# Letting the scheduler order TensorE's instructions in the layer 0 mixers of a two-layer hybrid backbone

## The chip, the cores and the metric

The program runs on one core of one Trainium2 chip. The metric is the device time of one execution in microseconds (us), the median of several runs. A profile of one execution stands beside it: the start and length of every instruction on the engines TensorE (PE, with its weight loads as PEld), VectorE (DVE), ScalarE (ACT) and GpSimd (POOL), and the transfers of the DMA queues.

## The reference, cut to what matters

640 tokens (128 of a context, 512 latent) of width 2048 go through two layers with a shared residual stream. Everything is float32.

```python
# per layer: (shift, scale, gate) = SiLU(cond) @ w_ada + b_ada ; h = RMSNorm(x) * (1 + scale) + shift
#            p = h @ w_in      (one projection for all head groups)
#            x = x + gate * ( concat(mixer_1(p) * silu(z_1), mixer_2(p) * silu(z_2)) @ w_out )
def delta_chunked(q, k, v, g, beta, s0):          # layer 0, mixer A: 8 heads, chunks of 64, both directions
    ...
    tmat = lmat + jnp.eye(CHUNK, dtype=F32)       # a triangular system in each chunk
    u = lax.linalg.triangular_solve(tmat, v * beta[..., None], ...)
    w = lax.linalg.triangular_solve(tmat, kb * jnp.exp(gc)[..., None], ...)
    def step(s, xs):                              # a serial scan over the chunks
        vn = ui - jnp.einsum('bhcd,bhde->bhce', wi, s)
        o = jnp.einsum('bhcd,bhde->bhce', qi * jnp.exp(gi)[..., None], s) + jnp.einsum('bhcs,bhse->bhce', ai, vn)
        s = s * jnp.exp(gl)[..., None, None] + jnp.einsum('bhcd,bhce->bhde', ki * ..., vn)
    ...
# layer 0, mixer B: 8 heads of windowed attention with a sink logit
# layer 1, mixers C (4 heads of gated linear attention) and D (8 heads of neighbourhood attention)
```

## The kernel before, in words

**Main work.** Each projection is cut into panels of 128 output columns; a panel is 16 blocks of 128 rows. Operands are split into a high and a low part, so that each block costs three matmuls of 320 tokens (`hh,w_hi`, `hl,w_hi`, `hh,w_lo`) for each half of the tokens, all adding up in a PSUM tile `acc`. A panel is thus 96 `acc` matmuls. Its weights come in quarters: a transfer into `w_st`, a cast on ACT into `w_hi` (L1048), a subtraction on DVE into `w_lo` (L1050); each of the three tiles has 3 buffers. `acc` has 3 buffers in PSUM, and a panel takes two of them. In layer 0, 53 panels make the mixers' inputs, and 16 more, the output projection, follow.

**The mixers of layer 0** run beside that main work as streams (Python generators, L1658 to L1733): convolutions, gates, preparation of a delta-net head (`a_prep`, L240), inversion of its triangular blocks on POOL (`a_invert`, L474, tiles `i_S`), joining the inverse (`a_join`), the serial scan (`a_scan`, L329), and the attention of a B head (`b_head`, L694, through `attn_run` and `attn_out`). A scan has ten steps for each head. A step first multiplies the state `a_s` by two stationary tiles (`a_st<-a_s,a_wT` and `a_st<-a_s,a_o`), ACT and DVE turn the result into `a_vno` (L411) and `a_vns` (L409), and TensorE then takes three products (`a_st<-a_r,a_Zt`, which belongs to the next step and reads `a_r` that ACT makes ahead, then `a_st<-a_vno,a_at` and `a_st<-a_vns,a_ktm`), from which DVE makes the next state (L426). In a B head each block of 128 queries has scores (`at_s`), a softmax, a transposition (`at_pt`), a copy on ACT into `at_P` (L614) and the product with the values (`at_o`).

**What sets the order.** The function `run` (L1202) is a planner that works while the program is written. It keeps an estimated time `g.now`, which each matmul advances, and the streams yield the time that they want to wait, from the table `LAT` (`hop=1.3` between two halves of a scan step, `pt=1.3` between `at_pt` and `at_o`, `inv=52` for an inversion). When no stream is due, `Main.step` issues three matmuls of main work. So the order in which matmuls are written interleaves scan steps with about a dozen `acc` matmuls each.

The framework then schedules the written program: at build time, with a timing model of its own, it gives out instructions as their inputs come free in that model, the earlier written one first among those that are ready. Each engine executes its own list in that order. Matmuls and transpositions go through two helpers (L74 and L83), which can tie each one behind the instruction of TensorE that was written before it:

```python
        i = self.nc.tensor.matmul(out, lhsT=lhsT, rhs=rhs, **kw)
        if self.pin:
            self.tc.keep_in_program_order(i)
```

With `g.pin` true, TensorE's list is the planner's order. It starts true (L1554), is set to false before the mixers of layer 1 (L1827), and is set to true in `out_proj` (L1535) after the first 14 panels of the output projection, ahead of the last two, which are done in halves. All other engines are ordered by the scheduler throughout.

After the mixers `out_proj` (L1502) finishes the output projection panel by panel: DVE adds each panel to the residual (`x`, L1518), and the vectors of the next layer's modulation (`ada_vec`, `scale` and `vec`, L1319) are computed on DVE, ACT and POOL as a filler.

Of the kernel before, what the change touches and what calls it, by code (L numbers as in the profile page):

```python
# [203 lines left out]
def a_conv(g, h, which, src):  # L204

    nc = g.nc
    pad = g.pad
    nc.scalar.copy(pad[:, 2:130], src[0][:, 0:128])
    nc.scalar.copy(pad[:, 134:326], src[0][:, 128:320])
    nc.scalar.copy(pad[:, 326:646], src[1])  # L210
    w = g.convw[:, which * 8 + h]
    y = g.pt.tile([128, CL], F32, name="a_y", tag="tmp")
    nc.vector.tensor_scalar_mul(y, pad[:, 0:CL], w[:, 0:1])
    for j in range(1, 5):
        nc.vector.scalar_tensor_tensor(out=y, in0=pad[:, j:j + CL], scalar=w[:, j:j + 1], in1=y,  # L215
                                       op0=ALU.mult, op1=ALU.add)
    t = g.pt.tile([128, CL], F32, name="a_t", tag="tmp")
    nc.scalar.activation(t, y, AF.Tanh, scale=0.5)
    o = (g.pa1 if which == 2 else g.pe).tile([128, T], F32, name=f"a_o{which}", tag=f"a_o{which}", bufs=(2, 2, 1)[which])
    nc.vector.scalar_tensor_tensor(out=o[:, 0:128], in0=t[:, 0:128], scalar=1.0, in1=y[:, 0:128], op0=ALU.add, op1=ALU.mult)  # L220
    for hf in range(2):
        nc.vector.scalar_tensor_tensor(out=o[:, 128:].rearrange("p (b a c) -> p a b c", a=2, c=64)[:, hf],
                                       in0=by_block(t[:, 132:], hf), scalar=1.0, in1=by_block(y[:, 132:], hf),
                                       op0=ALU.add, op1=ALU.mult)
    return o
# [332 lines left out]
def a_setup(g, es):  # L558

    nc, tc = g.nc, g.tc  # L560
    g.pa1 = es.enter_context(tc.tile_pool(name="pa1", bufs=1))
    g.paw = es.enter_context(tc.tile_pool(name="paw", bufs=1))
    g.Zt = [g.pa1.tile([128, 10, 64], F32, name=f"a_Zt{i}") for i in range(2)]
    g.pad = g.pa1.tile([128, CP], F32, name="a_pad")
    for z in g.Zt + [g.pad[:, 0:2], g.pad[:, 130:134], g.pad[:, 646:648]]:
        nc.gpsimd.memset(z, 0.0)
# [120 lines left out]
def b_query(g, h, qsrc):  # L687
    q = g.pb.tile([128, T], F32, name="b_q", bufs=2)
    drain(g, q, (yield from qsrc), SC)
    b_rope(g, q)  # L690
    return q
# [31 lines left out]
def b_setup(g, es):  # L723
    tc, nc = g.tc, g.nc
    g.pb = es.enter_context(tc.tile_pool(name="pb", bufs=1))
    t = g.pb.tile([128, 1536], F32, name="b_tab")
    nc.sync.dma_start(t, g.I["b_tab"])
    g.cos, g.sin, g.bmask = t[:, 0:512], t[:, 512:1024], t[:, 1024:1536]
# [473 lines left out]
def run(g, main, *streams):  # L1202


    live = [[s, None, g.now] for s in streams]
    while live:
        for e in live:
            if e[2] <= g.now if e[1] is None else e[1]():
                try:
                    y = next(e[0])  # L1210
                    e[1], e[2] = (y, 0) if callable(y) else (None, g.now + (y or 0))
                except StopIteration:
                    live.remove(e)
                break
        else:
            if not main.step():
                nn = min([e[2] for e in live if e[1] is None] + [main.when()])
                assert nn < INF
                g.now = nn
# [153 lines left out]
def ada_store(pool, n, k, width=512):  # L1373

    w = width // 4
    t = pool.tile([128, w + n * k * width], F32, name="adv")
    return t[:, 0:w], [t[:, w + j * k * width:w + (j + 1) * k * width] for j in range(n)]
# [169 lines left out]
def body(nc, tc, I, O):  # L1547
    off = [(k, v.shape[1]) for k, v in const_table().items()]
    with ExitStack() as es:
        g = G()  # L1550
# [99 lines left out]
        with ExitStack() as e1:  # L1650
            g.pt = pool(e1, "pt", 3)
            g.pz = pool(e1, "pz")
            g.pat = pool(e1, "pat")
            g.pss = pool(e1, "pss", 2, space=PSUM)
            g.psg = pool(e1, "psg1", 2, space=PSUM)
            a_setup(g, e1)
            b_setup(g, e1)
            g.spare = 8  # L1658
            main = Main(g, hh, hl, zip(EARLY, parts), slabs[-1][0])
            get = lambda n, prio, now=False: main.ask(W[n], prio, now, n)  # L1660
            prepped, inverted, values, gates, queried, bgates, st = {}, {}, {}, {}, {}, {}, dict(b=0, joined=-1, scanned=-1, ready={}, gates=False)

            tri = g.pe.tile([128, T], F32, name="g_tri", tag="a_o1", bufs=2)
            nc.sync.dma_start(tri[:, 0:512], I["a_tab"])

            def first():
                ps = yield from get(32, -1)
                gs = g.pe.tile([128, T], F32, name="gs", tag="a_o0", bufs=2)
                for i in range(2):
                    nc.scalar.copy(gs[0:64, i * 320:i * 320 + 320], ps[i][0:64])  # L1670
                yield LAT["drain"]
                yield from a_gates(g, gs, tri)
                st["gates"] = True

            def prep():
                for h in range(8):
                    yield lambda: st["joined"] >= h - 2
                    k = a_conv(g, h, 1, (yield from get(8 + h, 0.5)))
                    yield lambda: st["scanned"] >= h - 2
                    q = a_conv(g, h, 0, (yield from get(h, 0.5)))  # L1680
                    yield LAT["conv"]
                    yield lambda: st["gates"]
                    prepped[h] = yield from a_prep(g, h, q, k)
                    st["ready"][h] = g.now

            def value():
                for h in range(8):
                    yield lambda: st["joined"] >= h - 1 and h in st["ready"]
                    values[h] = a_conv(g, h, 2, (yield from get(16 + h, 1)))
                    yield LAT["conv"]  # L1690
                    values[h, 1] = True

            def zgate():
                for h in range(8):
                    yield lambda: st["scanned"] >= h - 1 and len(st["ready"]) >= h + 1
                    gates[h] = silu2(g, (yield from get(24 + h, 2)), g.pz, "zs_a")

            def inverses():
                for h in range(8):
                    yield lambda: st["joined"] >= h - 1 and h in prepped  # L1700
                    yield max(0, st["ready"][h] + LAT["inv"] - LAT["invld"] - g.now)
                    inverted[h] = a_inverted(g, h, *prepped[h]["inv"]), g.now

            def scans():
                for h in range(8):
                    yield lambda: (h, 1) in values and h in inverted
                    yield max(0, inverted[h][1] + LAT["invld"] - g.now)
                    prepped[h]["inv"] = inverted.pop(h)[0]
                    oT = yield from a_scan(g, prepped.pop(h), values.pop(h), gates, st)
                    g.outs.emit(h, oT)  # L1710
                    st["scanned"] = h

            def queries():
                for h in range(8):
                    yield lambda: len(st["ready"]) >= h and st["b"] >= h - 1
                    if h == 0:
                        yield from b_kv(g, 0, get(41, 3), get(43, 3))
                    queried[h] = yield from b_query(g, h, get(33 + h, 3))
                    st["q", h] = g.now

            def bgate():
                for h in range(8):
                    yield lambda: h in queried and st["b"] >= h - 1
                    bgates[h] = silu2(g, (yield from get(45 + h, 4)), g.pz, bufs=2)

            def bs():
                for h in range(8):
                    if h == 4:
                        yield from b_kv(g, 1, get(42, 0), get(44, 0))
                    yield lambda: h in queried  # L1730
                    yield max(0, st["q", h] + LAT["rope"] - g.now)
                    yield from b_head(g, h, queried[h], bgates)
                    st["b"] = h + 1  # L1733

            gate = ada(g, 0, (2,), [512] * (2048 // 512), ada_store(g.pa1, 1, 1, 512), 7)
            outs = g.outs = Outs(g, main, 53, I["w_out_even"], ORDER0, 2)
            run(g, main, inverses(), scans(), first(), prep(), value(), bs(), queries(), zgate(), bgate(), gate, outs.stream())
        e0.close()

# [233 lines left out]
```

## Time and profile before

| | |
|---|---|
| median of 3 runs | 2797.22 us (2791.26 to 2799.9) |
| the profiled execution | 2803.32 us, span 2801.5 us |
| PE busy | 2623.7 us (94%), 20855 matmuls |
| DVE busy | 1650.0 us (59%) |
| ACT busy | 998.2 us (36%) |
| POOL busy | 800.3 us (29%) |

Stages, in us from the start of the span: up to about 160 the modulation of layer 0 and the first panels; to about 1250 the layer 0 mixers with their main work; to about 1560 the output projection of layer 0; to about 2560 layer 1's mixers; then its output projection and the final norm.

A row of the windows view has the stretch, its length, the busy time of PE, PEld, DVE, ACT and POOL with the number of instructions in brackets, the mean granted clock of TensorE (1.00 is full speed), the DMA engines' share and GB/s. A row of the waits view has who waited for whom, the sum in us, how often, and the longest. A row of the timeline has the start and the length in us, engine, line, operation, output<-inputs, shapes and how many in a row; an idle time before it stands in square brackets with what ended it. A row of the chain that ended last, in order of time, has a start, a length and what ran. Matmuls overlap in the pipeline, so that the distance between starts, not the length, is what a matmul costs.

### The profile page before, as it was taken

What the parts mean: (1) busy time and instruction counts of PE and PEld (TensorE: products, weight loads), DVE (VectorE), ACT (ScalarE), POOL (GpSimd) and SP (SyncE); (2) the same over time, 40 slices, a digit from 0 to 9 for tenths busy, and PEclk for the clock granted to TensorE, in tenths of its full rate; (3) what the DMA queues carried; (4) which work ended last, traced back from release to release, by engine and by line L of the source; (5) the groups of instructions that cost most, each with busy time, mean ns of one, the idle gap of its engine ahead of it and who ended that gap; (6) DMA issues with size and microseconds to landing.
All of it is one profiled execution on the core that took longest, in us unless ns stands there. A gap on an engine that the chain in (4) does not pass through costs nothing.

```text
span 2801.5 us, 53986 instructions
## 1 busy us (share of the span) xinstructions
PE 2623.7 (94%) x20855; PEld 2458.3 (88%) x20855; DVE 1650.0 (59%) x3618; ACT 998.2 (36%) x2214; POOL 800.3 (29%) x946
## 2 busy tenths in 40 slices
PE   6889899999999999997979899999999999999997
PEld 5778787787878988997879799999999999999996
DVE  5765556565655664469998855454553636455225
ACT  3232342333333434353333543334324333343222
POOL 2326415053350550005554431013001201220223
PEclk9989999999999999998889999999999999999998
DMA  9933333332322222247665332232332323225334
GB/s 330 304 91 92 92 92 86 95 95 81 103 85 72 76 69 69 79 162 233 216 205 169 117 101 91 80 112 70 103 110 75 98 78 103 97 66 178 99 99 136
DMA packets 264705, 329.81 MB, mean 118 GB/s; under 512 B 76013, under 2 KB 148925, under 8 KB 264447
## 3 DMA queue, kind: packets, MB, share of 16 engines
q1 hardware_dynamic: 264447, 326.35, 36.8%
q8 instruction: 164, 2.69, 0.4%
q14 instruction: 94, 0.77, 0.1%
HBM read 294.95 MB, written 28.68 MB: 116 GB/s over the span
## 4 chain that ended last, share of the span: by engine, by line
PE 70%; DVE 10%; issue 9%; DMA 7%; POOL 2%; ACT 1%; SPq 1%; DVEq 0%; POOLq 0%; ACTq 0%
PE acc L77 55%; PE a_st L77 3%; DVE vec L1319 2%; DMA a_df<-gc_d 2%; PE at_s L77 2%; PE at_o L77 2%; DVE w_lo L1050 1%; PE ada_ps L77 1%; DVE scale L1319 1%; PE c_ops L77 1%; PE at_pt L84 1%; DMA adv<-w_ada 1%; PE c_lv L77 1%; POOL i_tmp L493 1%; POOL i_S L495 1%
## 5 line engine op out<-in xcount | busy, mean ns | idle before, releaser
L77 PE MATMUL acc<-hh,w_hi 128*128 128x320 f32 (+1 forms) x4544 | 1462.7, 323 | 53.4 <-DVE x L1518 42.5
L77 PE MATMUL acc<-hl,w_hi 128*128 128x320 f32 (+1 forms) x4544 | 1425.9, 314 | 9.1 <-DVE hl L1228 8.5
L77 PE MATMUL acc<-hh,w_lo 128*128 128x320 f32 x4480 | 1405.3, 314 | 11.5 <-DVE w_lo L1050 11.5
L77 PEld LDWEIGHTS acc<-hh,w_hi 128*128 128x128 f32 (+1 forms) x4544 | 866.2, 191 | 101.6 <-issue 73.5
L77 PEld LDWEIGHTS acc<-hl,w_hi 128*128 128x128 f32 (+1 forms) x4544 | 866.9, 191 | 14.7 <-DVE hl L1228 12.2
L77 PEld LDWEIGHTS acc<-hh,w_lo 128*128 128x128 f32 x4480 | 856.9, 191 | 14.4 <-DVE w_lo L1050 13.5
L1050 DVE TENSOR_TENSOR w_lo<-w_st,w_hi 128x512 fp32r<-128x512 f32 x561 | 435.9, 778 | 537.3 <-ACT w_hi L1048 532.0
L1048 ACT CAST w_hi<-w_st 128x512 fp32r<-128x512 f32 (+1 forms) x604 | 364.8, 604 | 835.8 <-PE acc L77 713.2
L1319 DVE SCALAR_TENSOR_TENSOR vec<-vec,cond 128x256 f32<-128x256 f32 (+1 forms) x360 | 248.8, 727 | 22.3 <-DMA vec<-w_ada 21.1
L495 POOL TENSOR_TENSOR i_S<-i_S,i_tmp 40x30 f32<-40x30 f32 (+14 forms) x240 | 144.6, 602 | 18.6
L493 POOL TENSOR_TENSOR i_tmp<-i_S 40x30 f32<-40x30 f32 (+14 forms) x240 | 136.6, 569 | 18.1
L1324 POOL TENSOR_TENSOR scale<-scale,scale_t 128x512 f32<-128x512 f32 x60 | 94.5, 1575 | 121.5 <-ACT scale_t L1322 61.7
L928 POOL TENSOR_TENSOR c_X<-c_b 128x320 f32<-128x320 f32 x56 | 46.9, 837 | 227.0 <-PE c_lv L77 199.6
L1462 POOL TENSOR_TENSOR n_acc<-n_acc,n_sq 128x640 f32<-128x640 f32 (+1 forms) x30 | 47.8, 1595 | 204.0 <-ACT n_sq L1461 204.0
L302 POOL TENSOR_TENSOR a_at<-a_df,consts 128x640 f32<-128x640 f32 x8 | 13.0, 1627 | 323.8 <-PE a_st L77 97.2
L789 POOL TENSOR_TENSOR d_bias<-d_braw,d_mask 128x256 f32<-128x256 f32 x32 | 28.5, 920 | 230.6 <-PE tm_ps L84 90.7
L77 PE MATMUL ada_ps<-adv,cond 128*32 128x128 f32 x1536 | 68.1, 299 | 25.2 <-DMA adv<-w_ada 23.6
L215 DVE SCALAR_TENSOR_TENSOR a_y<-a_pad,consts,a_y 128x644 f32<-128x644 f32 x96 | 90.1, 938 | 2.1
L77 PEld LDWEIGHTS ada_ps<-adv,cond 128*32 128x32 f32 x1536 | 39.2, 116 | 46.1 <-DVE n_acc L1462 19.6
L1322 ACT ACTIVATE scale_t<-scale,cond 128x512 f32<-128x512 f32 x60 | 43.0, 722 | 95.7 <-DMA scale<-w_ada 83.8
L1050 POOL TENSOR_TENSOR w_lo<-w_st,w_hi 128x256 fp32r<-128x256 f32 (+1 forms) x43 | 35.8, 838 | 105.2 <-ACT w_hi L1048 82.7
L593 ACT ACTIVATE at_S<-at_S,at_nm 128x384 f32<-128x384 f32 (+2 forms) x80 | 47.5, 594 | 49.9 <-DVE at_nm L591 49.6
(321 smaller groups left out, 2894.1 us busy)
## 6 DMA issues: line engine op xcount, KB each, us to landing
w_st<-w_in_odd SPq DMA_DIRECT2D x232, 256.0 KB
adv<-w_ada SPq DMA_DIRECT2D x192, 256.0 KB
w_st<-w_in_even SPq DMA_DIRECT2D x188, 256.0 KB
w_st<-w_out_even SPq DMA_DIRECT2D x72, 256.0 KB
w_st<-w_out_odd SPq DMA_DIRECT2D x72, 256.0 KB
scale<-w_ada SPq DMA_DIRECT2D x64, 256.0 KB
vec<-w_ada SPq DMA_DIRECT2D x64, 256.0 KB
vec<-w_ada SPq DMA_DIRECT2D x128, 128.0 KB
```

What stands on the lines that cost most here:

```text
L77: i = self.nc.tensor.matmul(out, lhsT=lhsT, rhs=rhs, **kw)
L215: nc.vector.scalar_tensor_tensor(out=y, in0=pad[:, j:j + CL], scalar=w[:, j:j + 1], in1=y, op0=ALU.mult, op1=ALU.add)
L493: E.tensor_tensor(out=t, in0=S[:, j + 1:, j].unsqueeze(2).to_broadcast([40, n, j]), in1=S[:, j, 0:j].unsqueeze(1).to_broadcast([40, n, j]) ...
L495: E.tensor_tensor(out=S[:, j + 1:, 0:j], in0=S[:, j + 1:, 0:j], in1=t, op=ALU.add)
L593: nc.scalar.activation(S[:, 0:n], S[:, 0:n], AF.Exp, bias=nm, accum_out=den[:, 0:1])
L928: nc.gpsimd.tensor_tensor(out=pv(X[0])[:, :, 1 - d], in0=bv[:, :, 1 - d], in1=bm, op=ALU.subtract)
L1048: nc.scalar.copy(hi, st)
L1050: (nc.gpsimd if g.spare >= 0 else nc.vector).tensor_tensor(out=lo, in0=st, in1=hi, op=ALU.subtract)
L1319: nc.vector.scalar_tensor_tensor(out=acc[:, c], in0=st, scalar=sc, in1=acc[:, c], op0=ALU.mult, op1=ALU.add)
L1322: nc.scalar.activation(t, st, AF.Copy, scale=sc)
L1324: nc.gpsimd.tensor_tensor(out=acc[:, c], in0=acc[:, c], in1=t, op=ALU.add)
L1462: eng.tensor_add(accs[0][:, cs], accs[0][:, cs], t[:, cs])
```

## The change

One line is added just before the planner runs the mixers of layer 0:

```diff
             gate = ada(g, 0, (2,), [512] * (2048 // 512), ada_store(g.pa1, 1, 1, 512), 7)
             outs = g.outs = Outs(g, main, 53, I["w_out_even"], ORDER0, 2)
+            g.pin = False
             run(g, main, inverses(), scans(), first(), prep(), value(), bs(), queries(), zgate(), bgate(), gate, outs.stream())
```

From there until `out_proj` sets it back (L1535 before the change), no matmul or transposition is tied to the one written before it. This covers the mixers and the first 14 panels of layer 0's output projection. No instruction is added or removed; the ties are gone, and the scheduler may issue a later written matmul first where, in its own timing model, the earlier one's inputs are not there yet.

## Prediction

> **What bounds the kernel now.** I read the page first, for the span, then the windows view, to see which stage has idle time on TensorE that another order could fill. The rows are the layer 0 mixers, the output projection after them, and the layer 1 mixers, whose TensorE list is already the scheduler's.
>
> ```profile
> span 2801.5 us, 53986 instructions
> 170.00:1230.00 1060.00, 1004.18 (x8639) 894.72 (x8640) 613.18 (x1545) 392.77 (x1009) 347.41 (x524) 0.97 0.29 86
> 1230.00:1560.00 330.00, 277.62 (x1831) 270.36 (x1830) 300.19 (x394) 118.59 (x202) 159.01 (x114) 0.90 0.62 201
> 1640.00:2560.00 920.00, 916.14 (x6847) 895.80 (x6847) 477.10 (x1166) 338.66 (x722) 153.10 (x161) 1.00 0.29 94
> ```
>
> In the layer 0 mixers TensorE is busy 1004.2 of 1060 us: it is the bound, and only 55.8 us are idle. In the layer 1 mixers it idles 3.9 of 920 us. In the stage between, DVE is busy 300.2 of 330 us. That stage also loses its ties, but its wait is another:
>
> ```profile
> PE acc L77 <- DVE x L1518: 42.5, 12, 8.0
> ```
>
> TensorE waits there for DVE to empty `acc`, and has nothing but further `acc` matmuls, which need the same three buffers. No order of TensorE's list fills that; I cost this stage at nothing. The cover is DVE's own queue; if DVE's list came out otherwise, some of the 42.5 us could move either way.
>
> Next, the waits of TensorE in the mixers, and one wait of DVE in the same window:
>
> ```profile
> PE a_st L77 <- ACT a_vno L411: 15.3, 5, 5.5
> PE a_st L77 <- DVE a_s L426: 7.1, 3, 3.7
> PE at_s L77 <- DVE a_at L321: 4.9, 1, 4.9
> PE at_s L77 <- ACT b_q L700: 3.6, 1, 3.6
> DVE a_df L301 <- DMA a_df<-gc_d: 35.4, 8, 5.2
> ```
>
> The first four make 30.9 of the 55.8 us. I read them as one cause. Each head's `a_prep` fetches `a_df`, DVE waits for it with 4.4 us on the mean (35.4 / 8), and behind that wait stand `a_vns`, the new state and the weights' `w_lo`. DVE's list is the scheduler's even now, and it put the subtraction at L301 where the transfer had not landed, in all eight heads. So the scheduler's timing model takes that transfer as sooner than it is, and will not see these stalls when it orders TensorE either.
>
> **The change part by part.** It removes ties and no work; TensorE still has 1004 us to do there. Three things can move: idle time that is filled, alternations between main and small matmuls, and the cover at the end of the mixers.
>
> *How the scheduler orders.* A matmul goes ahead of an earlier written one only when the earlier one is not ready in the model. Where the two layers share code, in the attention blocks, the planner asks for the same 1.3 us between `at_pt` and `at_o`. The chain in order of time, first layer 0, then layer 1:
>
> ```profile
> 361.81 0.44 PE at_pt L84 x4
> 362.25 1.76 PE acc L77 x12
> 364.00 0.89 PE at_o L77 x8
> ```
> ```profile
> 1720.31 0.33 PE at_pt L84 x3
> 1720.64 3.51 PE acc L77 x24
> 1724.15 0.67 PE at_o L77 x6
> ```
>
> With the ties there are 12 `acc` matmuls in that hop, without them 24. The model thus holds the hop to be longer than the planner does, and pulls later main work into it. That gives each hop more slack on the chip, which is the gain to expect. In layer 1's scan, what the same order looks like between two groups of state products is this:
>
> ```profile
> 1768.15 0.15 PE acc L77
> 1768.30 0.86 PE c_ops L77 x4
> 1769.16 0.15 PE acc L77
> ...
> 1773.36 0.59 PE acc L77 x4
> ```
>
> Single `acc` matmuls stand between the groups; the planner writes them in threes.
>
> *Idle time filled.* Of the 55.8 us, 30.9 us hang on `a_df` and stay, except for what the extra matmuls in a hop cover: four of them, as in the last row, are 0.59 us, in each of eight heads, 5 us. Of the other 24.9 us, which are short waits for several sources in the model's sight, I take half, 12 us. Bounds: nothing, and all 55.8 us. Together −17 us.
>
> *Alternations.* What a change from main to small matmuls and back costs is in the timeline of layer 0:
>
> ```profile
> 315.65 0.31 PE L77 MATMUL acc<-hl,w_hi 128*128 128x320 f32 x1
> 315.80 0.31 PE L77 MATMUL acc<-hh,w_lo 128*128 128x320 f32 x1
> 316.04 0.44 PE L77 MATMUL a_st<-a_s,a_wT 128*64 128x128 f32 x4
> 316.31 0.39 PE L77 MATMUL a_st<-a_s,a_o 128*64 128x128 f32 x4
> 316.63 0.41 PE L77 MATMUL acc<-hh,w_hi 128*128 128x320 f32 x1
> 316.88 0.31 PE L77 MATMUL acc<-hl,w_hi 128*128 128x320 f32 x1
> ```
>
> Inside a run the starts are 0.15 us apart. The last `acc` before the small group takes 0.24 (316.04 − 315.80), the first after it 0.25 (316.88 − 316.63). An alternation there and back costs 0.09 + 0.10 = 0.19 us. The Trainium skill, page TensorEngine Tiling (Array Packing), section Key Properties, says that changing the tiling mode drains TensorE, which speaks against finer alternation; every scan product here is tiled (128*64, 64*64, 64*128), so the rule puts a price on each further split of the scan and does not lower mine. How many more alternations there will be follows from the groups of the scan:
>
> ```profile
> L77 PE MATMUL a_st<-a_vno,a_at 64*64 64x128 f32 x320 | 32.8, 283 | 15.5 <-ACT a_vno L411 15.3
> L77 PE MATMUL a_st<-a_s,a_wT 128*64 128x128 f32 x288 | 32.7, 301 | 7.1 <-DVE a_s L426 7.1
> ```
>
> Four rows of the trace are one group, so there are 320 / 4 = 80 half steps in which `a_r`, `a_vno` and `a_vns` follow each other, and 288 / 4 = 72 in which the two products with the state do. `a_r` is made a step ahead, while `a_vno` and `a_vns` come from two engines at the end of the hop; `a_s` comes in two halves from two DVE instructions. With a hop that the model holds to be longer, `a_r`'s products go first and main work slips in before the others. I take one split for each of the 80 and for half of the 72: 116 × 0.19 = 22 us. Bounds: no split, 0 us; two for each of the 80 and one for each of the 72, 232 × 0.19 = 44 us. I take the middle because layer 1 has both whole groups and splits.
>
> *The cover at the end.* Main work that is pulled ahead is missing later. The mixers end with the last B head, where TensorE has little else:
>
> ```profile
> 1245.44 0.55 PE L84 MATMUL at_pt<-consts,at_S 128*128 128x128 f32 x3 [0.22 <-DVE at_S L602]
> 1248.44 0.94 PE L77 MATMUL at_o<-at_P,b_v 128*128 128x128 f32 x6 [1.58 <-ACT at_P L614]
> ```
>
> Even now this hop takes 3.0 us, of which 1.6 us are idle. If the other four blocks of that head lose their cover too, each adds such a stall once or twice: 4 × 1.58 = 6 us to 13 us. I take 9 us; bounds 0 and 13, since the head could also keep its cover.
>
> *Sum.* −17 + 22 + 9 = +14 us, so 2801.5 becomes 2815.5 in the span of the profiled execution and its 2803.32 us about 2817. The median of the runs lies 6.1 us below that execution, which gives 2811 us. With TensorE the bound, later stages only shift.
>
> The clock bears on the first term. After a stall it is slower for a while:
>
> ```profile
> 305.59 0.55 PE L77 MATMUL a_st<-a_vno,a_at 64*64 64x128 f32 x4 [3.18 <-ACT a_vno L411]
> ...
> 306.80 0.63 PE L77 MATMUL acc<-hh,w_hi 128*128 128x320 f32 x1
> 307.23 0.47 PE L77 MATMUL acc<-hl,w_hi 128*128 128x320 f32 x1
> ```
>
> The first `acc` after the stall takes 0.43 us instead of the 0.25 us above, and the granted clock over the window is 0.97 against 1.00 in layer 1. The Trainium skill, page TensorE: Matmul & The Clock Gate, section Part 1, states that an idle window of about 3.4 us halves the clock until about 3.4 us of work have passed; by that rule each stall of this length that is shortened gives back up to 1.7 us (an estimate from that page), and with five of them the sum would be about +6 us instead of +14. The trace agrees that the clock falls, and here already after 3.18 us. I leave the stalls on `a_df` in place, so nothing of this enters my sum.
>
> **The rivals.** *Faster: the mixers become as dense as layer 1's.* At layer 1's idle share, 3.9 / 920, the mixers would idle 4.5 us of 1060 and gain 51 us; with the 22 us of splits and no loss at the end that is −29 us, 2768 us; without the splits 2746 us. For it speaks that every hop gets more main work, so that DVE's late work on `a_vns` is covered whatever the model thinks of `a_df`. Against it speaks that layer 1 has no transfer in the middle of its scan on which DVE blocks. It decides from where the extra main work in a hop reaches the 4.4 us of that wait, some 30 `acc` matmuls at 0.147 us.
>
> *No change.* If the model sees hardly any stall in the planner's order, the list stays as it is, or gain and splits cancel: 2797 us. Against it: layer 1's rows above show that the model's hops differ from the planner's.
>
> *Much slower: the heads' chain becomes the bound.* If all 20 hops of a scan grow from 12 to 24 matmuls (1.76 to 3.51 us), a scan is 35 us longer. The main work between a scan's end and the next join would have to give way:
>
> ```profile
> 376.80 8.12 PE acc L77 x54
> ...
> 385.27 8.11 PE acc L77 x54
> ...
> 393.74 1.51 PE acc L77 x9
> ```
>
> These are 17.7 us, so 17 us for each of seven further heads would be uncovered: 122 us, 2919 us. Against it: main work that was pulled ahead is not lost, and the chip runs an uncovered hop faster than the model.
>
> **How the numbers follow.** A measurement of this kernel can tell about 0.3%, 8 us, from no change. Chances: my forecast (small loss from splits) 0.38, the dense rival 0.32, no change 0.20, the long chain 0.10. The first and last make slower 0.48. The range goes from 2760, with the dense rival's value inside, to 2858, where the bounds of my costs (+44 +13 with nothing filled, 2848) end and some of the long chain begins.
>
> **What would show it.** In the profile after, runs of `acc` that are not multiples of three, single `acc` matmuls between scan groups, at least a hundred more alternations, and 24 instead of 12 matmuls between `at_pt` and `at_o` would show the ordering as I read it. TensorE's idle time in the mixers should fall only to about 40 us, with `a_vno` and `a_s` still the longest waits and DVE's wait for `a_df` still near 35 us. If the idle time falls under 15 us, or the alternations do not grow, I am wrong towards faster; if TensorE idles more than now between scan steps or around the inversions, towards slower.

## The result, and the profile after

| | before | after |
|---|---|---|
| median | 2798.56 us (2791.26 to 2802.57, 4 runs) | 2872.07 us (2867.7 to 2874.05, 4 runs) |
| ratio | 1 | 1.0259, 95% interval 1.0245 to 1.0274 |
| span of the profiled execution | 2801.5 us | 2871.0 us |

The change costs 2.6%, 73.5 us in the medians and 69.5 us between the spans. Both stand outside the range of the prediction, on the slow side. First the windows view of the changed kernel: the stretch that the prediction quoted, and the output projection.

```profile
170.00:1230.00 1060.00, 984.78 (x8188) 859.71 (x8187) 563.60 (x1429) 357.73 (x923) 358.76 (x523) 0.94 0.27 79
1330.00:1680.00 350.00, 288.64 (x1864) 270.40 (x1865) 321.57 (x445) 128.93 (x230) 177.58 (x130) 0.91 0.60 193
```

In the mixers TensorE now idles 75.2 us (1060 − 984.78) where it idled 55.8, gets through 8188 matmuls instead of 8639 in the same time, and has a lower granted clock, 0.94 instead of 0.97. The mixers as a whole, from their first `gt_ps` to the last `at_o`, grew from 1086.7 to 1169.8 us, +83.1, with 108 more `acc` matmuls in them; the output projection behind has these 108 fewer and is 8.6 us shorter. So the loss arises in the mixers. What TensorE waits for there, and one wait of DVE (waits view, 160 to 1330 us):

```profile
PE a_ops L84 <- ACT a_oraw L456: 27.5, 6, 5.5
PE a_st L77 <- ACT a_vno L411: 8.9, 9, 2.0
PE acc L77 <- DVE zs_a L236: 7.7, 2, 5.3
...
PE a_st L77 <- DVE a_s L426: 5.4, 7, 1.7
...
DVE a_df L301 <- DMA a_df<-gc_d: 35.1, 7, 6.4
```

The waits that led before, `a_vno` and `a_s`, have shrunk, from 15.3 and 7.1 us to 8.9 and 5.4. At the top stands one that was not among the ten longest: `a_ops`, the transposition of a head's output after its scan and normalisation (L433 to L456). The chain in order of time shows where it comes from. First the end of the third head's scan before:

```profile
571.69 1.96 PE acc L77 x12
573.65 0.59 PE a_st L77 x8
574.24 1.51 PE acc L77 x9
...
580.11 1.96 PE acc L77 x12
582.06 0.39 PE a_st L77 x4
...
590.13 1.26 ACT a_oraw L456 x4
```

and the same place after:

```profile
634.23 0.79 PE a_st L77 x8
635.02 3.27 PE acc L77 x21
638.29 0.95 PE a_st L77 x12
639.25 4.30 PE acc L77 x28
643.55 0.79 PE a_st L77 x8
644.34 2.54 PE acc L77 x16
646.87 0.61 PE a_st L77 x8
...
649.54 0.18 DVE a_rt L450
...
652.42 0.41 ACT a_oraw L456
652.88 1.36 PE a_ops L84 x4
...
660.41 1.71 PE acc L77 x9
```

Before, each hop here has 9 or 12 `acc` matmuls, and while the normalisation runs on DVE and ACT, from 582.3 us to the start of `a_ops` at 594.4, TensorE starts 42 `acc` matmuls beside it. After, the hops hold 21 and 28, and from 646.6 us, when the last of the 16 starts, no main matmul starts until 660.1. The last hop, the whole normalisation and a block of a B head run bare (without main matmuls beside them).

The following table counts this in the two timelines, summed over the eight heads. "Join" runs from the inverse's first product to the scan; the scan is cut in thirds of its time; "norm" runs from behind its last product to about the last `a_ops`; "rest" from there to the next join. In each pair the first number counts `acc` matmuls, the second is lost time in us: the distance from each TensorE instruction's start to the next one's, less the lower quartile of that distance for the same tile in the kernel before. A distance counts where it starts, so the idle time between a scan's last product and `a_ops` stands in the scan's last third (27.5 of the 95 us after), not in norm. The total also has what lies ahead of the first join and behind the last head, the output projection included.

```
             join      scan 1/3   scan 2/3   scan 3/3   norm      rest      total lost
before       444  40   547  70    445  77     565  58   510  21  1094   9   420
after        547  29   715 108    989  66    1001  95   160  12   394  28   494
```

A scan grew from 57.2 us on the mean to 83.9, and the main work in the eight scans from 1557 `acc` matmuls to 2705. It took this main work from behind: norm and rest had 1604 matmuls and have 554; in six of the eight heads none at all stands between the scan's last product and `a_ops`. The lost time grew by 74 us, as much as the kernel.

The bare ends are the larger part of that, not all of it. The last third, norm and rest lose 47 us more (37 − 9 + 19; the rest runs at the lower clock that a bare end leaves behind, as shown further down). The first third loses 38 us more, of which 10 us stand behind `a_wps`, which had its place in the join before, 9 us behind `a_gram`, of which 520 now fall there instead of 280, and 13 us behind `acc`. Join and middle third lose 11 us less each, and 11 us lie outside the table's columns.

### The profile page after: what moved, and what is told of

Read it like the earlier page. It is cut to its first block, busy times and chain, and to the rows that moved or that the text cites. A ratio compares the mean times of both kernels' runs of the same rounds, so it can differ in the third digit from the quotient of the medians.

```text
span 2871.0 us, 53925 instructions
## 1 busy us (share of the span) xinstructions
PE 2665.0 (93%) x20855; PEld 2474.7 (86%) x20855; DVE 1639.6 (57%) x3618; ACT 995.6 (35%) x2214; POOL 810.9 (28%) x946
## 4 chain that ended last, share of the span: by engine, by line
PE 75%; DVE 10%; DMA 6%; issue 5%; POOL 3%; ACT 1%; SPq 1%; DVEq 0%; ACTq 0%; POOLq 0%
PE acc L77 59%; PE a_st L77 4%; DVE vec L1319 2%; PE at_o L77 2%; PE at_s L77 2%; DMA a_df<-gc_d 2%; POOL i_S L495 1%; PE ada_ps L77 1%; POOL i_tmp L493 1%; DVE w_lo L1050 1%; PE at_pt L84 1%; DMA adv<-w_ada 1%; PE c_ops L77 1%; PE c_lv L77 1%; DMA vec<-w_ada 1%
## 5 line engine op out<-in xcount | busy, mean ns | idle before, releaser
L77 PE MATMUL acc<-hh,w_hi 128*128 128x320 f32 (+1 forms) x4544 | 1439.8, 318 | 37.4 <-DVE x L1518 14.2
L1319 DVE SCALAR_TENSOR_TENSOR vec<-vec,cond 128x256 f32<-128x256 f32 (+1 forms) x360 | 247.3, 725 | 18.1 <-DMA vec<-w_ada 16.6
L495 POOL TENSOR_TENSOR i_S<-i_S,i_tmp 40x30 f32<-40x30 f32 (+14 forms) x240 | 153.7, 640 | 18.8
L664 POOL TENSOR_TENSOR b_sw<-b_sw,b_tab 128x512 f32<-128x512 f32 x10 | 14.9, 1489 | 282.8 <-DMA b_sw<-b_q 252.5
L426 DVE SCALAR_TENSOR_TENSOR a_s<-a_s,g_egl,a_st 128x128 f32<-128x128 f32 x128 | 39.8, 342 | 59.0 <-PE a_st L77 58.8
```

Source lines behind the costliest of these rows:

```text
L426: nc.vector.scalar_tensor_tensor(out=sn[:, d], in0=s[:, d], scalar=hs(A["egl"][hf])[:, o, blk:blk + 1], in1=ds, op0=ALU.mult, op1=ALU.add)
L495: E.tensor_tensor(out=S[:, j + 1:, 0:j], in0=S[:, j + 1:, 0:j], in1=t, op=ALU.add)
L1319: nc.vector.scalar_tensor_tensor(out=acc[:, c], in0=st, scalar=sc, in1=acc[:, c], op0=ALU.mult, op1=ALU.add)
```

## The experiments

**The theories.** A, the prediction's dismissed rival: longer hops make the heads' chain longer, and that alone is the loss. A2: the scheduler's model takes a hop of the scan as about twice as long as the planner does, and fills each with main work that was written as cover for something later; where no further main work can come forward, the chain runs bare. B in the expectations is the prediction's own finer alternation, C a loss outside the scans. A2 was put only after the first four runs (ties in the scans, free scans, long hops, main matmuls tied), so that it explains those afterwards and foretells the others. The rivals to A2 place the loss in the free order itself (splits, small products, buffers, the output projection). All kernels compute the same; only order, ties or buffers differ.

**Ties in the scans alone.** The change, with ties while a scan's ten steps are written:

```diff
+    g.pin = True
     for i, (o, blk) in enumerate(order):
         s, p = yield from step(o, blk, s, p, order[i + 1] if i < 9 else None)
...
+    g.pin = False
```

> The change, but with the ties back while the ten steps of a scan are written (all matmuls written then, main work among them). Theory A, long hops: the free order puts 21 to 28 main matmuls into each half step of a scan instead of 12, so a scan takes 76 to 96 us instead of 58, and that is where the 72 us come from. A expects scans of 58 to 65 us and 2795 to 2825 us. Theory B, the finer alternation of my prediction: most of the scan's splits are gone, so B expects about the same as A here. Theory C, the loss lies outside the scans or in the lists of the other engines: 2850 to 2875 us.

Measured: 2801.12 us (2794.56 to 2804.73) against 2798.49 before, ratio 1.001 [0.9999, 1.0022]. The whole loss is gone, though everything outside the scans stays free. What the freed order does to the joins, the preparation, the B heads and the output projection sums to about nothing. That is a sum of two parts: the free output projection alone gains 7 us (below), so the rest costs about 10 (an estimate from these two ratios). Main work pulled ahead out of that projection gains little there: the stage takes 350.0 us here with 1668 `acc` matmuls, and 347.8 us with 1750 in the kernel with free seams at the end of this section.

**Free scans alone.** The counterpart: the kernel before, with `g.pin = False` ahead of that loop and `True` behind it.

> The kernel before, with the ties off only while the ten steps of a scan are written. Theory A (long hops in the scan): scans of 75 to 90 us and 2840 to 2875 us. Theory B (finer alternation): at least 100 more changes between main and small matmuls than before, and the loss in proportion, 0.19 us each. Theory C (loss outside the scans): 2795 to 2815 us.

Measured: 2894.78 us (2892.58 to 2902.49), ratio 1.0353 [1.0331, 1.0374]. Freeing only the scans costs more than the change, 96 us, and above A's range of 2840 to 2875 us, though the scans take 71 us, less than A's 75 to 90. The end of the same head's scan in this kernel's timeline, TensorE alone:

```profile
606.29 0.44 PE L77 MATMUL a_st<-a_vno,a_at 64*64 64x128 f32 x4 [1.37 <-ACT a_vno L411]
606.66 0.49 PE L77 MATMUL a_st<-a_vns,a_ktm 64*128 64x128 f32 x4
607.66 0.43 PE L77 MATMUL a_st<-a_s,a_wT 128*64 128x128 f32 x2 [0.50 <-DVE a_s L426]
...
610.70 0.44 PE L77 MATMUL a_st<-a_vno,a_at 64*64 64x128 f32 x4 [1.66 <-ACT a_vno L411]
...
613.74 0.69 PE L77 MATMUL a_st<-a_vno,a_at 64*64 64x128 f32 x4 [0.77 <-ACT a_vno L411]
620.03 1.65 PE L84 MATMUL a_ops<-consts,a_oraw 128*128 128x128 f32 x5 [5.60 <-ACT a_oraw L458]
```

From 604 to 620 us there is not one main matmul. The main work from `a_ops` on is tied behind it here and cannot come forward, so what was written up to there is all there is: scan and norm together have 2019 `acc` matmuls, where they had 2067 (table below). The first two thirds of the scan take 1560 of them instead of 992, the work written beside the normalisation among them. The last third has 435 (565 before) and norm 24 (510 before), and the last third loses 153 us (58 before), 44 of them idle ahead of `a_ops`, while the middle third, with 899 instead of 445, loses less than before. That is A2 in its plainest form.

**Long hops, all tied.** The kernel before, but the planner itself writes hops as long as the freed scheduler makes them:

```diff
-        yield LAT["hop"]
+        yield LAT["hop"] + 2.2
...
-        yield LAT["hop2"]
+        yield LAT["hop2"] + 1.2
```

> The kernel before, all ties kept, but the planner is told that the two halves of a scan step last 3.5 and 2.7 us (hop plus 2.2, hop2 plus 1.2), so that it writes about 27 and 21 main matmuls into them as the free order does. Theory A: the length of the hops is the cause whoever orders them: scans of 80 to 90 us, 2840 to 2880 us. Theory B: fewer, longer runs of main work, no loss: 2790 to 2805 us. Theory C (what the freed scheduler does besides): 2795 to 2810 us.

Measured: 2807.1 us (2804.7 to 2810.78), ratio 1.0029 [1.0018, 1.004]. The first seven scans last 88 to 96 us, longer than in the changed kernel, and the cost is 8.6 us, not 73. So A fell: long scans by themselves cost a small part at most. A planner that knows of them moves other work beside them (the B heads end at 1172 us, ahead of the last scan, which runs beside the output projection, in 55 us).

**Only the main matmuls tied, and only the others tied.** Two halves of the freedom. In the first the main matmuls stay tied to one another and the small ones are free; in the second it is the other way round.

```diff
-        if self.pin:
+        if self.pin is True or self.pin == ("main" if main else "small"):
...
-            g.pin = False
+            g.pin = "main"
```

> The change, but each main matmul stays tied behind the matmul written before it; only the small ones of the streams are free. Theory A: main work can no longer overtake a scan product that is not ready in the model, the hops stay at 12, scans 58 to 65 us, 2790 to 2820 us. Theory B: small products still move among main work and split it: 2820 us or more. Theory C (small products overtaking main work and each other): 2850 us or more.

> The change, but all TensorE instructions other than the main matmuls stay tied to one another in program order; the main matmuls alone are free. Theory A2 needs only main matmuls that overtake scan products which are not ready in the model: nearly the whole loss stays, 2850 to 2890 us, with 20 or more acc matmuls in the early hops. Rival S (the small products that change places among themselves, of heads, preparations and attention, cost the time): 2800 to 2820 us.

Measured: 2824.26 us (2818.53 to 2837.49), ratio 1.0103 [1.007, 1.0135], and 2882.55 us (2880.04 to 2884.32), ratio 1.0293 [1.0278, 1.0309]. With free main matmuls and the small ones in program order the whole loss is there, and some more: it is the main matmuls that overtake. Tying only them leaves a third of the loss, just above what A had foretold (2820 us); the hops mostly hold 12 main matmuls again, and which small products cost that third was not tried.

**Long hops, free.** The change and the two lines of the long hops together.

> The change, and in it the planner asks for longer hops in the scans of layer 0 (hop + 2.2 us, hop2 + 1.2 us), so that it writes about as many acc matmuls into each hop (20 to 27) as the freed scheduler puts there by itself. Theory A2 (cover spent early: the scheduler takes a hop as about twice as long as it is and fills the early hops of a scan with main work that was written for the late ones and for the normalisation): now each hop has been written with as much as the scheduler wants, nothing has to be pulled ahead, and the time falls back near the long hops with ties, 2800 to 2825 us, with the wait of a_ops for a_oraw under 12 us in sum. Rival F (the free order itself costs, through splits, main work at the wrong moment or a worse order of the small products): 2860 us or more. Rival L (longer scans as such): 2870 us or more, though the long hops with ties already speak against it.

Measured: 2842.51 us (2839.84 to 2848.91), ratio 1.0154 [1.0137, 1.0171]. None of the forecasts held. With hops written as long as the model wants them, the wait of `a_ops` is nearly gone and 30 of the 73 us with it, as A2 says:

```profile
PE a_ops L84 <- ACT a_oraw L456: 4.1, 1, 4.1
PE a_st L77 <- DVE a_s L426: 10.8, 10, 3.3
```

But 35 us stay above the long hops with ties, 23 of them in the first third of the scans (91 us lost against 68 with ties).

**Room for the next gate.** In the changed kernel main work waits at times for `zs_a` (L236), which has one buffer: the gate of the next head can't be emptied out of `acc` before the present head has used its own. Here both gates share a tag with three buffers.

```diff
-                    gates[h] = silu2(g, (yield from get(24 + h, 2)), g.pz, "zs_a")
+                    gates[h] = silu2(g, (yield from get(24 + h, 2)), g.pz, bufs=3)
...
-                    bgates[h] = silu2(g, (yield from get(45 + h, 4)), g.pz, bufs=2)
+                    bgates[h] = silu2(g, (yield from get(45 + h, 4)), g.pz, bufs=3)
```

> The change, and the gates of the two groups of heads share one tag with three buffers, so that the gate of the next A head (zs_a) has room before the scan in progress has used its own. Rival Z (the freed main work stops at the single buffer of zs_a, and that is why the ends of the scans are bare): the DVE wait of zs_a (L236) for its buffer, 13.9 us in sum in the changed kernel, goes, the ends are filled, 2835 us or less. Theory A2 (the scheduler spends the cover early by its own timing, whatever buffers there are): that wait goes or shrinks, but the scans stay at 75 us or more with bare ends, 2850 to 2880 us.

Measured: 2867.97 us (2860.46 to 2874.55), ratio 1.0241 [1.0215, 1.0267]. A2's time held, but not its bare ends: the buffer decides where the bare stretch lies, though not how much is lost.

```profile
PE ada_ps L77 <- DMA adv<-w_ada: 14.1, 8, 5.8
PE a_ops L84 <- ACT a_oraw L456: 4.3, 2, 4.1
```

The ends are covered now (norm has 527 `acc` matmuls instead of 160, the wait of `a_ops` is 4.3 us), and the bare stretch stands in the joins and at the start of the scans: the join has 351 instead of 547, and the first third loses 121 us.

**Ties in half of each scan.** The change, with ties in the last five steps, and with ties in the first five:

```diff
     for i, (o, blk) in enumerate(order):
+        if i == 5:
+            g.pin = True
...
+    g.pin = False
```
```diff
+    g.pin = True
     for i, (o, blk) in enumerate(order):
+        if i == 5:
+            g.pin = False
```

> The change, but the ties are on during the last five of the ten steps of each scan. Theory A2 in the form that the cover runs out: the free first five steps use 20 to 28 acc matmuls a hop where 12 were written, and the ties keep them from drawing on what is written behind; about half of their hops come out bare, so half of the loss of the free scan (96 us) stays: 2825 to 2850 us. Rival E (the loss lies in the last steps themselves, in the order that the scheduler gives them): tying them repairs it, 2815 us or less.

> The change, but the ties are on during the first five of the ten steps of each scan. Theory A2 in the form that the cover runs out: the ten free hops draw some 120 acc matmuls more than were written there, and behind a scan stand about 200 for each head (norm and rest) that they can draw on, so little is lost: 2800 to 2825 us. Rival E (the loss lies in the last steps themselves): it stays, 2840 us or more.

Measured: 2838.48 us (2836.54 to 2844.16), ratio 1.0142 [1.0119, 1.0164], and 2863.43 us (2858.46 to 2868.26), ratio 1.0227 [1.0202, 1.0252]. The first is as A2 foretold: about half of the loss, and it lies just ahead of the first tied step. The timeline of the fourth head there:

```profile
680.05 0.44 PE L77 MATMUL a_st<-a_vno,a_at 64*64 64x128 f32 x4 [1.31 <-ACT a_vno L411]
680.42 0.49 PE L77 MATMUL a_st<-a_vns,a_ktm 64*128 64x128 f32 x4
681.42 0.43 PE L77 MATMUL a_st<-a_s,a_wT 128*64 128x128 f32 x2 [0.51 <-DVE a_s L426]
...
687.53 0.47 PE L77 MATMUL a_st<-a_s,a_wT 128*64 128x128 f32 x1 [5.31 <-DVE a_s L426]
```

From step 2 to step 5 most hops are bare, and DVE's wait for `a_df`, 4.79 us there, now shows in full: TensorE idles 5.31 us behind it, with no main work in front. The second missed: I took it that the late steps could draw on the main work behind the scan at no cost. They did draw on it, and the last third lost less than before (52 us, 58 before), but the shortage moved on to the next join, just ahead of the next tied step. Its chain there:

```profile
406.87 1.21 PE i_vps L77 x40
408.08 1.04 PE a_tps L84 x4
409.12 1.05 PE i_zps L77 x40
...
411.43 1.13 PE a_tps L84 x4
...
413.70 2.00 PE a_wps L77 x8
415.70 0.62 PE a_st L77 x4
416.32 2.70 PE acc L77 x9
```

A whole join without a main matmul; over the eight heads the joins have 61 of them where they had 444. The join's last products, `a_wps`, already fall into the next scan's first third here, where they alone lose 16.6 us; that is part of the 125 us there. The kernels side by side, counted as above:

```
             join      scan 1/3   scan 2/3   scan 3/3   norm      rest      total lost
before       444  40   547  70    445  77     565  58   510  21  1094   9   420
after        547  29   715 108    989  66    1001  95   160  12   394  28   494
scans tied   329  32   504  82    486  82     615  59   685   7   941  10   419
scans free   456  48   661  84    899  52     435 153    24  13  1120  18   517
end tied     571  24   457  90    272 119     623  60   687   7   939  10   458
start tied    61  57   604 125    903  77    1027  52   646   4   438  19   488
small tied   620  27   846  87   1031  64     814 124    57  22   343  28   506
gates' room  351  42   584 121    918  73    1036  64   527  14   470  13   488
long, tied   444  40   994  68    919  86     859  80   555  14   403   6   429
long, free   599  29   909  91    906  92     864  86   519   8   353  16   460
```

In the kernels with a known wall the column that loses is the one just ahead of it: the end of the scan (scans free), the sixth step (end tied), the next scan's first step (start tied: the join and the first third, into which the join's end falls).

**Long hops, free, first five steps tied.** The change, the two lines of the long hops, and the ties of the first five steps together.

> The change with the long hops of the planner, and the ties on during the first five steps of each scan. The long hops without ties stood 35 us above the long hops with ties, 23 of them in the first third of the scans. Theory M (that remainder is the small products of other streams, a_gram, ada_ps and a_wps, set between the scan products of the early hops): 2805 to 2822 us. Rival N (the remainder is a loss of all free hops, or of the seams between the scans): 2832 us or more.

Measured: 2825.04 us (2822.13 to 2826.8), ratio 1.0089 [1.0069, 1.0109]. Between the two forecasts: ties in the early steps bring back 17 of the 35 us. What causes the other 18 stays open.

**The free output projection, and a version to beat both.** The kernel before with one line behind `run(...)`, and the kernel before with that line and free seams between the scans (`g.pin = True` at a scan's start, `g.pin = h == 7` at its end):

```diff
             run(g, main, inverses(), scans(), first(), prep(), value(), bs(), queries(), zgate(), bgate(), gate, outs.stream())
+            g.pin = False
```

> The kernel before, with the ties off only from the end of the planner's run, that is in the first 14 panels of the output projection. Theory A2 says that the loss arises in the scans: 2798 us, within 0.3%. Rival O (part of the loss arises in the output projection, where the waits of acc change from the sum x to w_lo): 2806 us or more.

> The kernel before, but free of ties where the scheduler's order looked harmless: from the end of each scan to the start of the next, and in the output projection; the scans, the stretch before the first and the B heads after the last stay tied. Theory A2 places the whole loss in the free scans: no slower than before, and with the 7 us that the free output projection gave, 2780 to 2795 us. Rival N (free seams cost too): 2800 us or more.

Measured: 2792.36 us (2783.07 to 2794.45), ratio 0.9968 [0.9953, 0.9983], and 2790.75 us (2782.64 to 2794.6), ratio 0.9973 [0.9958, 0.9988]. The free output projection is a small gain, not a loss: the stage went from 357.9 to 348.8 us, 4 of these 9 us for 28 `acc` matmuls fewer. Its waits only changed their names, here in the kernel with the one line (1245 to 1610 us):

```profile
PE acc L77 <- DVE w_lo L1050: 45.0, 20, 6.7
PE acc L77 <- DVE x L1518: 0.6, 2, 0.3
```

Free seams add nothing to it that can be measured. Both beat the two kernels, by 0.3%.

## Why the prediction was wrong

The mechanism that it read from layer 1, main work pulled ahead into each hop, was right, and so were two of its signs. What it had wrong is what that does: it put the missing cover at one place, the last B head, where the runs show it at the scans. The same hop of a B head after:

```profile
411.10 0.33 PE at_pt L84 x3
411.43 3.52 PE acc L77 x24
414.95 0.67 PE at_o L77 x6
```

There are 24 matmuls where there were 12, as foretold; most runs of `acc` are no multiples of three any more (167 of 277 between 170 and 1230 us); and DVE's wait for `a_df` stands at 35.1 us, as the prediction left it. What failed are three terms of the sum.

**"I take one split for each of the 80 and for half of the 72: 116 × 0.19 = 22 us."** Wrong in sign. The changes between main and small matmuls in the mixers fell from 660 to 598. With twice as many matmuls in a hop there are hops with none in exchange, and these take away more changes than the splits add. The price of an alternation holds in the trace before (0.24 and 0.25 us around 0.15, as the median of over 120 cases each); there were no more of them to pay. The prediction's sentence on the Trainium skill's rule that a change of tiling mode drains TensorE so bears on a cost that did not arise.

**Idle time filled, −17 us.** Instead 19.4 us more (75.2 − 55.8), and 26 us over the whole mixers. The waits on `a_vno` and `a_s` did fall by 8.1 us, about half of the 5 + 12 us that were counted on, but `a_ops` alone added 27.5. The prediction's own sign of being wrong towards slower, more idle time than before, is there.

**"Main work that is pulled ahead is missing later", and the place where.** This was the right sentence, applied at one place only, to the last B head at +9 us. That head and the ones beside it, behind the last scan, lost 16.8 us against 13.4, so +3.4. The place that mattered is the scans: their ends, bare in six of the eight heads, with the slow stretch behind them at +47 us, and their first thirds at +38. The rival "the heads' chain becomes the bound" had the ends, at 2919 us with a chance of 0.10, and was set aside with "main work that was pulled ahead is not lost, and the chip runs an uncovered hop faster than the model". The second half is true (a bare pair of hops takes 1.66 + 0.79 us in the kernel with ties in the last five steps, as medians, against 2.42 + 2.16 before with 12 matmuls in each), but TensorE does nothing in most of that time, and main work that isn't lost shortens the kernel later only if something is there to be covered by it.

The rival's number comes near by luck. With the scans' measured growth of 26.7 us instead of 35, its own arithmetic leaves 9.0 us a head uncovered, 63 us for its seven heads. But its 17.7 us of cover are three rows of the chain view, and the table has 1604 `acc` matmuls in norm and rest before, some 29 us a head at 0.147 us each (an estimate), more than the growth: by that count no head would be uncovered. The cover was there in sum; it stood in the wrong place, and the long hops with ties show that a long scan can be covered when the order is written for it. Two sums of the prediction are also slightly off, which changes nothing: 7 × 17.3 is 121 us, not 122, and its upper bound of the costs is 2797 + 57 = 2854 us, not 2848.

The clock went the other way too: the prediction left it out of its sum, and its sentence on the clock reckoned only with a gain. The transposition after a scan (tile view; durations in ns as shortest/median/longest), before, after, and with free scans:

```profile
L84 PE MATMUL a_ops<-consts,a_oraw x40: 270/273/331, 369.8 to 1139.9; 128*128 128x128 f32 x40
```
```profile
L84 PE MATMUL a_ops<-consts,a_oraw x40: 270/474/477, 406.1 to 1238.7; 128*128 128x128 f32 x40
```
```profile
L84 PE MATMUL a_ops<-consts,a_oraw x40: 473/476/477, 381.1 to 1230.1; 128*128 128x128 f32 x40
```

Behind the bare end of a scan these take 474 ns instead of 273. The Trainium skill, page TensorE: Matmul & The Clock Gate, section Part 1, has the clock at half after an idle window of about 3.4 us; the trace agrees, with waits of 4.1 to 6.8 us ahead of `a_ops` in the kernel with free scans and all 40 of its transpositions at 473 ns or more. So each bare end also slows what follows it. By the granted clock in the two traces TensorE stood at half clock for 137 us of the mixers, where it was 72 us; 96 us of that it was busy, where it was 61. At half speed that is some 17 us of the loss (an estimate from these two figures), beside the 26 us of idle time.

What is shown: the free order of the scans makes the loss (ties there remove it, freedom there alone makes it), main matmuls overtaking makes at least most of it, long scans as such do not, and in the kernels with a known wall the bare stretch lies ahead of it. What stays open: which obstacle stops the main work in the changed kernel once the gates have room, what the first third loses beyond the products that moved into it, and the 18 us of the free long hops that ties in the first five steps don't bring back.

## What to carry to other kernels

Work that is written as cover for a serial chain is a budget, made with one estimate of the chain's steps; a scheduler with a longer estimate spends the same budget early and leaves what comes later bare. Before giving an order free, compare the two estimates for each kind of step, multiply by the number of steps, and look for what is bare then at the end of every chain, not only at the end of the stage. The ties can be kept for the chain alone and dropped elsewhere; the stretch that suffers is the one just ahead of the next tie or full buffer.

## What the runs showed of the hardware beyond that

With ties in the last five steps, the hops with nothing but the scan's own products took 1.66 us from the last product with the state to the first with `a_vno`, 1.24 of them idle (median of 8), and 0.79 us from the last product with `a_vns` to the next with the state, 0.49 of them idle (median of 15). The freed order most often puts 28 and 21 `acc` matmuls there, 4.30 and 3.27 us, over three and over six times the idle time. The planner's waits of 1.3 and 1.5 us are near the chip or above it.

A change from main matmuls to small ones does not always cost the same. In the kernel before, at the full clock, the last `acc` ahead of a group of `a_st` (tiled, such as `128*64`) takes 0.24 us to the next start, but ahead of `at_o`, `at_pt` or `at_s` (all `128*128`) it takes 0.15, as inside a run. The first `acc` behind takes 0.25 and 0.23 us. So of the prediction's 0.19 us some 0.08 is paid for any small group, and 0.11 more for a tiled one.
